# Out layer 0: the last weight quarter three steps behind the third instead of six

## The chip, the cores and the metric

One Trainium2 chip, one core. The metric is the device time of one execution in microseconds (us), the median of three runs. All times below are us from the start of the profiled execution's span, unless they are called a duration.

## What is computed

One inference step of a two-layer decoder trunk: 1024 prompt rows and 8 sample rows, width 1024, all in float32. Layer 0 mixes by stick-breaking attention and causal pooling, layer 1 by a Conformer convolution. Each layer ends in an output projection and a normalisation of the residual sum:

```python
h = concat([o_a * silu(g_a), o_b * silu(g_b)])      # layer 0's mixed rows, 1024 wide
x = layer_norm(ALPHA * x + h @ w_out, g, b)         # what is called "out layer 0" here
p = x @ w_in_c                                      # layer 1 begins with its input projection
```

The sample rows attend to 4096 cached positions each, through a page table. Their scores need one product of every cached K row with the query, spread over the whole of layer 0 as a background job.

## The kernel before

A projection is computed in three matmuls per block, because operands are split into a high part (float32r) and the rest: `XH` by `whi`, `XH` by `wlo`, `XL` by `whi`. TensorE (PE), VectorE (DVE), ScalarE (ACT) and GpSimd (POOL) run in the order in which the code issues their instructions (`manual_schedule` names these four). SyncE (SP), which issues all DMAs, is ordered by the framework's planner.

`out_layer` works in 32 steps. A step is a pair (weight quarter `n4`, row tile `tb`): 24 matmuls of 128x128 by 256 columns, then on DVE the residual sum (L1073) and its statistics (L1077). Steps 0 to 15 do quarters 0 and 1 for all tiles. After that quarter 2 runs over the tiles, and quarter 3 follows `lag` steps behind it:

```python
for i in range(NTB + lag):
    if i < NTB:
        order.append((2, i))
    if i >= lag:
        order.append((3, i - lag))
```

With `lag` 6 the steps from 16 on are (2,0) to (2,6), (3,0), (2,7), (3,1), (3,2) to (3,7). The two accumulators of PSUM alternate, so a step's matmuls wait until DVE has taken up the result of the step before the last.

The step of quarter 3 completes a row tile. Then:

- in the step itself, DVE aggregates the statistics (L1005) and POOL makes the reciprocal deviation `rs` (L1007, L1008);
- one step later (`DTC`) the normalisation `app`: two DVE instructions (L1015) against `gps0`, a copy of the gain in PSUM, one ACT scaling (L1031), one POOL addition of the bias (L1032), and a DMA of the rows to `x1_dram` (L1137). Tile 7 is normalised on DVE alone (L1024, L1025), in the same step as tile 6, with two PSUM banks of the `zt` ring as its place between;
- `FLAG` steps after that (3 for tiles 0 to 4) `fin0`: eight PE transposes (L1144) into two `zt` banks, and from there ACT (L195, `XH`) and DVE (L196, `XL`) make layer 1's operands.

`tail0` issues the loads of layer 1's first four weight blocks (`wraw`) at (3,2) to (3,5), and converts them at (3,4) to (3,7): ACT `whi` L205, POOL `wlo` L210. Quarter 3's own four blocks are loaded at steps 13 to 16 and converted at steps 16 to 19, whatever the lag.

After each step `tick(1)` moves the background job `decode_k` on by one unit: DVE reduces unit u-3 (L409), POOL or DVE multiplies unit u-2 (L417, every fourth one is DVE's), SP loads unit u (`kt`, L405, four buffers). Unit 63's multiplication stands in step 24, its reduction in step 25, the score transposes and ACT's four sigmoids (L429 to L434) in step 28, the two scans (L437, L440) in steps 29 and 30. So within a step the order on each engine is: conversion, step, statistics, `decode_k`, then what `point()` finds due.

Layer 1's input projection `c_gen` follows at once. Its first block needs `XH` and `XL` of tiles 0 to 3. After six of its matmuls come tile 4's transposes. The four `zt` banks of out layer 0 are replaced at that point by a pool with two (`swap_psum("pzc", 2)`).

Of the kernel before, what the change touches and what calls it, by code (L numbers as in the profile page):

```python
# [69 lines left out]
TSLOPE = 1.5  # L70
NHEADS = (0, 6, 6, 6, 6, 6, 6, 6)
SNY = 7
OLAGB = 6
FDMA = (2, 3, 4, 5)
FC = (4, 5, 6, 7)
FLAG = (3, 3, 3, 3, 3, 4, 6, 8)
# [24 lines left out]
def kernel(  # L101
# [33 lines left out]
    def psum(tag, bufs, shape=(P, 512), dt=F32):  # L135
        return (psq[0] if tag == "qv" else ps).tile(list(shape), dt, tag=tag, name=tag, bufs=bufs)
# [338 lines left out]
    def tick(n):  # L475
        while n > 0 and queue:
            try:
                next(queue[0])
                n -= 1
            except StopIteration:  # L480
                queue.pop(0)
# [626 lines left out]
    def load_res(tb):  # L1108
        if tb < NTB:
            sp.dma_start(X[tb], xp[tb * P:(tb + 1) * P, :])  # L1110

    def before0(n4, tb):
        if n4 == 0:
            load_res(tb + 2)
        if n4 == 0 and tb == 4:
            sp.dma_start(pool_sample[0, :, 0:PS_ - 1, :], state_pool[0, :, 1:PS_, :])
            sp.dma_start(conv_sample[0, :, 0:KS - 1, :], state_conv[0, :, 1:KS, :])
        if n4 == 1 and tb == 0:
            sp.dma_start(gb0[:, 0, :], ln_ab_g.to_broadcast([P, D]))
            sp.dma_start(gb0[:, 1, :], ln_ab_b.to_broadcast([P, D]))  # L1120
        if n4 == 2 and tb == 4:
            gps0.extend((psum("o", 1), psum("qv", 1)))
            for i in range(2):
                act.activation(out=gps0[i], in_=gb0[:, 0, i * 512:i * 512 + 512], func=AF.Copy)
# [11 lines left out]
    def fin0(tb, y, h):  # L1136
        sp.dma_start(x1_dram[tb * P:(tb + 1) * P, h], y[:, h])  # L1137

        def f():
            for hf in range(h.start // 512, h.stop // 512):  # L1140
# [10 lines left out]
    load_res(1)  # L1151
    out_layer(w_out0, first0, ahead0, X, [gb0], lnp, fin0,
              lambda n4, tb: tick(0 if n4 == 0 and tb < 4 else 2 if n4 == 1 and tb < 4 else 1), before0, None, tail0, OLAGB, FASTB, WIDE, gps0)
    def v_tile():
        return cd.tile([P, HW], F32, tag="vt", name="vt", bufs=VB)
# [553 lines left out]
```

## Time and profile before

| what | value |
|---|---|
| device time, median of 3 runs | 1108.89 us (1107.83 to 1113.12) |
| the profiled execution: its own time, its span | 1105.15 us, 1103.4 us |
| PE busy | 1038.9 us, 94% of the span |
| DVE busy | 827.3 us, 75% |
| POOL busy | 628.5 us, 57% |
| ACT busy | 493.3 us, 45% |
| DMA | 235.20 MB, mean 213 GB/s |

The span is the time from the first to the last instruction on the chip. Shares of the whole span average over stages with different limits; the change touches steps 18 to 28 of out layer 0, which lie between some 523 and 557 us, and what follows them.

### The profile page before, as it was taken

What the parts mean: (1) busy time and instruction counts of PE and PEld (TensorE: products, weight loads), DVE (VectorE), ACT (ScalarE), POOL (GpSimd) and SP (SyncE); (2) the same over time, 40 slices, a digit from 0 to 9 for tenths busy, and PEclk for the clock granted to TensorE, in tenths of its full rate; (3) what the DMA queues carried; (4) which work ended last, traced back from release to release, by engine and by line L of the source; (5) the groups of instructions that cost most, each with busy time, mean ns of one, the idle gap of its engine ahead of it and who ended that gap; (6) DMA issues with size and microseconds to landing.
All of it is one profiled execution on the core that took longest, in us unless ns stands there. A gap on an engine that the chain in (4) does not pass through costs nothing.

```text
span 1103.4 us, 19870 instructions
## 1 busy us (share of the span) xinstructions
PE 1038.9 (94%) x6804; PEld 835.9 (76%) x6804; DVE 827.3 (75%) x982; ACT 493.3 (45%) x933; POOL 628.5 (57%) x490
## 2 busy tenths in 40 slices
PE   8999999999999999989978999999999899789996
PEld 7998888888889788979966665567566466677785
DVE  3468998899578979678882799999999950584246
ACT  5355675575765567601162244535542412462211
POOL 3366867665266778768683276647754612342135
PEclk9999999999999899989989999999999999999998
DMA  8678767865357676487534886876787688386923
GB/s 266 202 216 237 249 193 221 251 181 177 115 157 215 201 261 209 152 293 246 168 136 143 256 256 213 262 246 201 214 262 241 205 246 266 109 282 216 333 96 135
DMA packets 179350, 235.20 MB, mean 213 GB/s; under 512 B 15434, under 2 KB 95955, under 8 KB 179225
## 3 DMA queue, kind: packets, MB, share of 16 engines
q1 hardware_dynamic: 179249, 233.94, 67.1%
q8 instruction: 53, 0.87, 0.3%
q14 instruction: 48, 0.39, 0.1%
HBM read 212.60 MB, written 16.14 MB: 207 GB/s over the span
## 4 chain that ended last, share of the span: by engine, by line
PE 50%; DVE 9%; POOL 8%; DMA 7%; issue 5%; ACT 3%; SPq 2%; POOLq 0%; DVEq 0%; ACTq 0%
PE acc L225 11%; PE acc L227 10%; PE acc L226 10%; PE qv L1169 6%; DMA kt<-in_cache_k_dram 3%; POOL kt L417 3%; DVE zw L409 2%; POOL wlo L210 2%; DVE kp L365 2%; PE o L865 2%; PE acc L1040 1%; DMA vt<-in_cache_v_dram 1%; PE qv L1205 1%; PE zt L849 1%; DVE kt L417 1%
## 5 line engine op out<-in xcount | busy, mean ns | idle before, releaser
L225 PE MATMUL acc<-xh,whi 128*128 128x384 f32 (+2 forms) x960 | 360.9, 376 | 9.3 <-ACT xh L195 6.4
L227 PE MATMUL acc<-xl,whi 128*128 128x384 f32 (+2 forms) x960 | 339.7, 354 | 0.5 <-DVE xl L196 0.5
L226 PE MATMUL acc<-xh,wlo 128*128 128x384 f32 (+2 forms) x960 | 339.4, 354 | 0.0
L417 POOL TENSOR_TENSOR kt<-kt,qbs 128x1024 f32<-128x1024 f32 x96 | 232.7, 2434 | 78.5 <-DMA kt<-in_cache_k_dram 66.2
L210 POOL TENSOR_TENSOR wlo<-wraw,whi 128x512 fp32r<-128x512 f32 x124 | 167.7, 1356 | 168.9 <-ACT whi L205 163.6
L1391 DVE SCALAR_TENSOR_TENSOR conv_acc<-hbuf,wdwT,conv_acc 128x1024 f32<-128x1024 f32 x196 | 252.8, 1290 | 6.8
L225 PEld LDWEIGHTS acc<-xh,whi 128*128 128x128 f32 x960 | 183.2, 191 | 76.0 <-issue 25.7
L227 PEld LDWEIGHTS acc<-xl,whi 128*128 128x128 f32 x960 | 183.1, 191 | 18.5 <-DVE xl L196 1.1
L226 PEld LDWEIGHTS acc<-xh,wlo 128*128 128x128 f32 x960 | 183.8, 191 | 16.1 <-POOL wlo L210 0.2
L409 DVE TENSOR_REDUCE zw<-kt 128x16 f32<-128x1024 f32 x128 | 153.1, 1212 | 31.6 <-POOL kt L417 26.5
L1381 POOL TENSOR_TENSOR conv<-conv,tap 128x512 f32<-128x512 f32 x84 | 105.9, 1294 | 17.9 <-ACT tap L1378 17.9
L205 ACT ACTIVATE whi<-wraw 128x512 fp32r<-128x512 f32 x126 | 77.6, 625 | 72.4 <-DMA wraw<-in_w_out_ab_dram 53.3
L1040 PE MATMUL acc<-whi,xh 128*128 128x256 f32 x352 | 102.7, 292 | 5.0 <-DVE xres L1073 4.9
L1042 PE MATMUL acc<-whi,xl 128*128 128x256 f32 x352 | 99.7, 283 | 2.4 <-DVE xl L196 2.4
L1041 PE MATMUL acc<-wlo,xh 128*128 128x256 f32 x352 | 99.7, 283 | 1.1 <-POOL wlo L210 1.0
L365 DVE TENSOR_TENSOR_SCAN kp<-kp,zt 128x512 f32<-128x512 f32 (+3 forms) x96 | 92.6, 964 | 3.0 <-ACT zt L361 2.9
L1378 ACT ACTIVATE tap<-hbuf,wdwT 128x512 f32<-128x512 f32 x84 | 59.7, 721 | 48.3 <-POOL conv L1381 38.4
L1169 PE MATMUL qv<-vt,zw 128*32 128x512 f32 x512 | 75.0, 604 | 4.6 <-DMA vt<-in_cache_v_dram 4.6
L1040 PEld LDWEIGHTS acc<-whi,xh 128*128 128x128 f32 x352 | 67.1, 190 | 13.7 <-issue 7.4
L360 ACT ACTIVATE kp<-zt,nbiash 128x512 f32<-128x512 f32 (+3 forms) x96 | 55.8, 581 | 46.1 <-PE zt L827 24.4
L1042 PEld LDWEIGHTS acc<-whi,xl 128*128 128x128 f32 x352 | 67.1, 191 | 2.6 <-DVE xl L196 2.6
L1041 PEld LDWEIGHTS acc<-wlo,xh 128*128 128x128 f32 x352 | 67.1, 191 | 1.5 <-POOL wlo L210 1.5
(287 smaller groups left out, 1488.1 us busy)
## 6 DMA issues: line engine op xcount, KB each, us to landing
kt<-in_cache_k_dram SPq DMA_DIRECT2D x256, 256.0 KB
vt<-in_cache_v_dram SPq DMA_DIRECT2D x256, 256.0 KB
wraw<-in_w_in_c_dram SPq DMA_DIRECT2D x48, 256.0 KB
vt<-in_w_in_c_dram SPq DMA_DIRECT2D x48, 256.0 KB
wraw<-in_w_in_ab_dram SPq DMA_DIRECT2D x46, 256.0 KB
xt<-in_x_prompt_dram SPq DMA_DIRECT2D x8, 512.0 KB
wraw<-in_w_out_ab_dram SPq DMA_DIRECT2D x16, 256.0 KB
xres<-in_x_prompt_dram SPq DMA_DIRECT2D x8, 512.0 KB
```

The source lines that it names most:

```text
L210: (eng or gp).tensor_tensor(out=lo, in0=raw, in1=hi.bitcast(F32), op=ALU.subtract)
L225: pe.matmul(o, hi[:, k % 4, :], xh, start=(k == 0), stop=False)
L226: pe.matmul(o, lo[:, k % 4, :], xh, start=False, stop=False)
L227: pe.matmul(o, hi[:, k % 4, :], xl, start=False, stop=(k == NK - 1))
L365: dve.tensor_tensor_scan(out=kr, data0=kr, data1=z[:, 0:1].broadcast_to([P, n]), initial=1.0 if prev is None else prev, op0=ALU.mult, op1= ...
L409: dve.tensor_reduce(out=seg[:, j // 8, j % 8:j % 8 + 2, bi * 8:bi * 8 + 8], in_=kts.pop(s - KLAG - 1).rearrange("p a (h d) -> p a h d", d=DH),
L417: eng.tensor_tensor(out=kt, in0=kt, in1=qrow[b], op=ALU.mult)
L1040: pe.matmul(o, XH[:, k, cs], hi[:, k % 2, :], start=(k == 0), stop=False)
L1041: pe.matmul(o, XH[:, k, cs], lo[:, k % 2, :], start=False, stop=False)
L1042: pe.matmul(o, XL[:, k, cs], hi[:, k % 2, :], start=False, stop=(k == NK - 1))
L1169: pe.matmul(pv[32 * bi:32 * bi + 32, :], Z[:, j % 8 * 4 + j // 8, :], vts[bi], start=(j == 0), stop=(j == NPG - 1), tile_position=(0, 32 * ...
L1391: dve.scalar_tensor_tensor(out=part[1], in0=hb[:, j:j + S], scalar=w, in1=part[1], op0=ALU.mult, op1=ALU.add)
```

## The change

The lag of out layer 0 becomes 3. The steps from 16 on are now (2,0) to (2,3), (3,0), (2,4), (3,1), (2,5), (3,2), (2,6), (3,3), (2,7), (3,4) to (3,7). Steps 28 to 31 hold the same pairs as before. (3,0), (3,1), (3,2) and (3,3) move from steps 23, 25, 26 and 27 to 20, 22, 24 and 26. The normalisations of tiles 0 to 3 come at the ends of steps 21, 23, 25 and 27 instead of 24, 26, 27 and 28, that of tile 4 stays at 29, and the transposes of tiles 0 to 3 come at the ends of steps 24, 26, 28 and 30 instead of 27, 29, 30 and 31. The first two loads of layer 1's weights are issued in steps 24 and 26 of the code instead of 26 and 27. The copy of the gain to PSUM moves from (2,4), which was step 20, to (2,2), which is step 18, so that it still stands ahead of the first normalisation. `decode_k` keeps its place, one unit after each step.

```diff
-OLAGB = 6
+OLAGB = 3
...
-        if n4 == 2 and tb == 4:
+        if n4 == 2 and tb == 2:
             gps0.extend((psum("o", 1), psum("qv", 1)))
             for i in range(2):
                 act.activation(out=gps0[i], in_=gb0[:, 0, i * 512:i * 512 + 512], func=AF.Copy)
```

## Rows read from the trace of the kernel before

**Rows 1.** Busy us of each engine by stretch, granted clock, DMA share, GB/s.
```profile
536.00:548.00 12.00, 12.00 (x104) 12.00 (x103) 9.98 (x16) 0.00 (x0) 7.93 (x5) 1.00 0.41 142
...
573.00:580.00 7.00, 3.48 (x10) 2.52 (x10) 5.78 (x11) 4.51 (x8) 6.83 (x9) 0.66 0.62 216
```
**Rows 2.** Timeline, PE: start, duration, line, output and inputs, idle before and releaser.
```profile
574.74 0.80 PE L225 MATMUL acc<-xh,whi 128*128 128x512 f32 x1 [5.95 <-ACT xh L195]
...
580.02 0.66 PE L1144 MATMUL zt<-ident,xres 128*128 128x128 f32 x4 [1.79 <-DVE xres L1025]
```
**Rows 3.** Chain that ended last, in order of time, around the end of out layer 0.
```profile
574.04 2.37 POOL xres L1032
576.41 1.25 POOL wlo L210
...
577.93 0.58 POOL rs L1008
578.56 1.42 DVE xres L1025 x2
...
584.36 0.40 PE acc L225
584.76 0.24 PE acc L226
```
**Rows 4.** Timeline, POOL.
```profile
530.49 1.28 POOL L210 TENSOR_TENSOR wlo<-wraw,whi 128x512 fp32r<-128x512 f32 x1
531.74 2.39 POOL L417 TENSOR_TENSOR kt<-kt,qbs 128x1024 f32<-128x1024 f32 x1
537.27 4.76 POOL L417 TENSOR_TENSOR kt<-kt,qbs 128x1024 f32<-128x1024 f32 x2 [3.14 <-DMA kt<-in_cache_k_dram]
```
**Rows 5.** Timeline, DVE.
```profile
536.43 0.41 DVE L1073 SCALAR_TENSOR_TENSOR xres<-xres,acc 128x256 f32<-128x256 f32 x1
...
537.23 1.20 DVE L409 TENSOR_REDUCE zw<-kt 128x16 f32<-128x1024 f32 x1
...
546.52 1.22 DVE L417 TENSOR_TENSOR kt<-kt,qbs 128x1024 f32<-128x1024 f32 x1
547.65 0.74 DVE L1015 SCALAR_TENSOR_TENSOR xres<-xres,mv,o 128x512 f32<-128x512 f32 x1
...
548.97 0.41 DVE L1073 SCALAR_TENSOR_TENSOR xres<-xres,acc 128x256 f32<-128x256 f32 x1
...
549.88 0.26 DVE L1005 BATCH_NORM_AGGREGATE mv<-st 128x2 f32<-128x24 f32 x1
...
564.96 1.29 DVE L196 TENSOR_TENSOR xl<-zt,xh 128x512 fp32r<-128x512 f32 x2 [1.39 <-ACT xh L195]
...
568.64 1.21 DVE L440 TENSOR_TENSOR_SCAN kpd<-kpd 128x512 f32<-128x512 f32 x1
```
**Rows 6.** Timeline, ACT.
```profile
559.17 1.28 ACT L433 ACT_TABLE_LOAD   x1
560.47 0.69 ACT L433 ACTIVATE kpd<-zt,nbiasd 128x512 f32<-128x512 f32 x1
...
562.76 1.17 ACT L1031 ACTIVATE xres<-xres,rs 128x1024 f32<-128x1024 f32 x1
563.80 0.64 ACT L205 ACTIVATE whi<-wraw 128x512 fp32r<-128x512 f32 x1
564.33 1.10 ACT L195 ACTIVATE xh<-zt 128x512 fp32r<-128x512 f32 x2
```
**Rows 7.** Timeline, POOL, then DVE: a DVE multiplication while POOL multiplies.
```profile
510.44 2.40 POOL L417 TENSOR_TENSOR kt<-kt,qbs 128x1024 f32<-128x1024 f32 x1 [0.90 <-DMA kt<-in_cache_k_dram]
...
511.03 2.90 DVE L417 TENSOR_TENSOR kt<-kt,qbs 128x1024 f32<-128x1024 f32 x1
```
**Rows 8.** Timeline, SP: DMA issues.
```profile
528.19 4.00 SPq L200 DMA_DIRECT2D wraw<-in_w_in_c_dram  x2
532.78 6.52 SPq L405 DMA_DIRECT2D kt<-in_cache_k_dram  x8
```

## The prediction

> **What bounds the kernel now.** I read the page first, then the busy time by stretch, the timelines of PE, DVE, POOL, ACT and SP from 505 to 600 us, and the chain that ended last. PE is busy 94% of the span, but that is a mean. Up to about 548 us PE has no idle time in out layer 0, and DVE is already at 83% of it, with `decode_k` beside it [rows 1]. The end of the stage is another place: from 573 to 580 PE has 3.48 us of 7, at a granted clock of 0.66, while POOL has 6.83 and DVE 5.78 [rows 1]. PE waits 5.95 us for tile 3's `XH`, then 1.79 us for L1025, tile 7's last step on DVE [rows 2]. The chain says why L1025 is late: POOL adds tile 5's bias, makes a `wlo`, makes tile 7's `rs`, and only then can L1025 run [rows 3]. So what counts is when L1025 ends, 579.98 now; layer 1 follows from there, with PE on the chain.
>
> The tile 4 transposes that wait for it (580.02) don't read tile 7. They use a `zt` bank, and the pool of two that has just replaced the pool of four lays its second bank over the one that L1025 reads. The change makes as many `zt` allocations in the same order at the end (tiles 2 and 3, then tile 7), so I take this wait to stay.
>
> **The change part by part.** No instruction is added or removed. The sum is a walk through the four fixed orders: an instruction starts when its engine is free and its input is done (0.06 us later, the rows' usual distance). Durations, start to start: result and statistics 0.8 us (536.43 to 537.23) [rows 5], with aggregation 1.05; reduction 1.15; normalisation on DVE 1.32 (two L1015), on ACT 1.15, on POOL 2.38; `xl` pair 1.21; scan 1.21; `rs` pair 0.85 (end of `wlo` to end of `rs`); `wlo` 1.27; POOL's multiplication 2.38, DVE's 1.15 [rows 3 to 6]. Walked with them, the old order ends L1025 at 579.8, row 579.98; that is the error that I claim for the method where nothing new enters.
>
> *Weights and the gain.* Quarter 3's last `wlo` ends at 531.77 [rows 4]. (3,0) is now step 20, which starts at 529.0 and wants this block after three quarters of its 2.86 us, at 531.2: 0.6 us of PE, inside DVE's lag (its next result is taken up at 536.4), so it costs nothing. ACT waits for loads around steps 16 to 20, and the two copies of the gain fall into that at no cost. If that cover were gone they would cost some 1.2 us (512 columns each, as the `whi` of 0.64) [rows 6].
>
> *Tile 0's normalisation now meets `decode_k`.* Up to 538.35 DVE and POOL go as in the old rows [rows 4, 5]. Then DVE normalises tile 0 to 539.7, ACT to 540.9, POOL adds to 543.3 and does tile 1's `rs` to 544.15. Behind them in POOL's queue stands the multiplication of unit 61, which used to start at 539.65, the second of the two in its row [rows 4]. It now ends at 546.5, and DVE, in order, has to wait for it with its reduction, having nothing left since 542.65: 3.9 us of DVE idle. POOL itself stood idle from 539.6 to 540.9 for ACT. This is the core of my forecast: a normalisation crosses DVE, ACT and POOL, and what is queued behind its last part on POOL is the work that DVE needs next. In the old order it came at step 24, when POOL's last multiplication was past.
>
> *Tile 1's meets DVE's last multiplication.* DVE goes on: reduction to 547.7, tile 1's normalisation to 549.05, result and aggregation to 550.1, reduction to 551.25, then unit 63's multiplication, while POOL adds tile 1's bias from 550.3 to 552.7. A DVE multiplication alone took 1.22 us [rows 5]; one that began inside a POOL multiplication took 2.90 and ended 1.07 after POOL's did [rows 7]. The same here would end it at 553.8 instead of 552.4: 1.4 us. Below, 0 if a bias addition doesn't do what a multiplication does; above, the whole 1.68 between the two rows. I take 1.4, since both are POOL instructions of two SBUF operands and 2.4 us. The Trainium skill, SBUF — State Buffer, section "SBUF: two separate sides", has this as an exclusive lock of a port pair between a DVE operation with two SBUF inputs and a GpSimd operation that reads SBUF, whichever starts first. The 2.90 agrees. By that page the 1.4 us is due, without it the sum is 1.4 less.
>
> *Steps 24 to 28.* Tile 0's `xl` to 555.0, step 25's result to 555.8, the last reduction to 556.95, tile 2's normalisation to 558.3, step 26 to 559.3, tile 1's `xl` (after ACT) 560.05 to 561.3, step 27 to 562.1, tile 3's normalisation to 563.4, step 28 to 564.45. PE waits for DVE's results meanwhile, some 2 us at step 26 and under 1 us at steps 27 to 31.
>
> *The sigmoids.* In step 28 ACT has tile 3's scaling to 564.6, the table load to 565.9 and four sigmoids (2.29 us) to 568.2 [rows 6]. Tile 2's transposes now come in this step, so `xh` is behind the sigmoids, `xl` behind `xh`, and everything on DVE behind `xl`, which starts at 568.8: 4.3 us idle. In the old rows the same block held up tile 1's `xl`, with 1.39 us of DVE idle [rows 5], since tile 3's normalisation and a scan lay ahead of it.
>
> *The end.* DVE from 568.8 has no idle time to speak of: `xl`, step 29, scan, tile 4's normalisation to 573.6; step 30, scan, tile 3's `xl` to 577.15, tile 5's normalisation to 578.5. Tile 5 passes ACT at 579.7 and POOL at 582.1, `wlo` is at 583.4, tile 7's `rs` at 584.2, L1025 ends at 585.65, and the transposes start at 585.7. That is **5.7 us later** than 580.02 (4.3 without the port's 1.4). What was moved out of the end, one normalisation and one `xl` of DVE (2.5 us), is more than used up by the waits.
>
> *Clock.* After the 5.95 us idle PE ran at 0.43 us a matmul of 512 columns, the lower level (1.2 GHz), until 584.4, then at 0.24 [rows 2, 3]. Now it idles about 3.5 us before layer 1 and 6.6 before the tile 4 transposes. As long a slow stretch after 585.7 as there was after 574.74 (9.6 us instead of the 3.9 left after 580.5) costs 5.7 x (1 - 0.24/0.43) = 2.5 us more; none, if it lasts only as long as before. I take the middle, 1.3.
>
> *Moved DMAs.* The rows of tiles 0 to 3 are written earlier; their writes become ready after all K loads, so I leave them behind these in SP's queue. Layer 1's first weight loads already stand ahead of the last K loads in SP's queue, and held them to 532.78 [rows 8]; waiting for the same `wlo` as before, they cost the same.
>
> **Sum.** 4.3 + 1.4 + 1.3 = 7.0 us, 0.6%. The profiled execution took 1105.15 (span 1103.4 and 1.75 around it), so 1112.15 like for like; the median of the runs stands 3.7 above it, so 1115.9. The likeliest case's own range is 4.3 + 0 + 0 to 4.3 + 1.7 + 2.5: 1113.2 to 1117.4.
>
> **Rivals.** *The spacing pays* (the other side): DVE loses neither 3.9, 1.4 nor 4.3 us, as would be if POOL and ACT were done in time at steps 23 to 28. For it: two steps are 5.7 us, and a tile needs 3.2 of POOL and 2.5 of DVE. Against it: the queues are fixed and unit 61 stands behind tile 0. L1025 would come 3.9 us early, the slow stretch costs up to 1.7 less: 1108.9 - 3.9 - 1.3 = 1103.7. It decides once unit 61's multiplication starts by 540.
>
> *Nothing arrives at the end*: later stages take up the delay, for instance where K's successor, the V pages, sets the pace. For it: the chain passes a few V loads, 3 to 4 us each. Against it: PE stands on the chain from 580 on. 1108.9.
>
> *SP reorders*: tile 0's write, ready at 543.3, is put ahead of K unit 61's load. That unit would land some 4.4 us later, at 547.8 instead of being waited for until 544.15: 3.7 us more, 1119.6. Against it: every K load is free to go before that write is.
>
> **Chances.** Forecast 0.52, of which 0.36 above the bound (the sum lies 1.5 us beyond it) and 0.16 below; SP reorders 0.13; nothing arrives 0.20; spacing pays 0.15, about half of it beyond the bound. 0.5% of the time, 5.5 us, is about what a measurement of this kernel tells from no change. Slower 0.49, within 0.43, faster 0.08. The range goes from 1105.5, which leaves out most of the case that pays, to 1120.5, past the SP case.
>
> **What would show it.** In the changed profile: POOL's L1032 of tile 0 between two multiplications of units 60 and 61, and a DVE idle near 4 us before L409 at about 546; a DVE multiplication near 2.6 us around 551; a DVE wait of about 4 us for ACT's `xh` in step 28, near 568; PE's tile 4 transposes waiting for L1025 until about 585.7. It is wrong if unit 61 isn't behind tile 0, if the wait for L1025 is gone (`zt` banks laid otherwise), or if the end comes before 580.

## The result: 1117.09 us, 0.84% slower

| | before | after |
|---|---|---|
| device time, median | 1108.89 us (1104.20 to 1113.12, 7 runs) | 1117.09 us (1113.59 to 1121.08, 7 runs) |
| ratio of the runs, as recorded (the medians alone give 1.0074) | | 1.0084, 95% interval 1.0065 to 1.0102 |
| profiled execution: span | 1103.4 us | 1114.5 us |

The two profiled executions differ ahead of the change already: quarter 3's last `wlo`, from the same instructions, ends at 531.77 before [rows 4] and at 534.59 after. So I count from there below: **after minus 2.8 us** is the forecast's own time.

Busy time by stretch, after (busy us of PE, PEld, DVE, ACT, POOL, granted clock, DMA share, GB/s):
```profile
536.00:548.00 12.00, 12.00 (x104) 12.00 (x104) 9.08 (x15) 1.15 (x1) 8.16 (x8) 1.00 0.67 226
548.00:556.00 8.00, 6.16 (x42) 5.96 (x42) 6.42 (x8) 2.12 (x3) 6.45 (x4) 0.84 0.05 20
...
580.00:590.00 10.00, 2.44 (x13) 1.63 (x12) 7.12 (x13) 4.01 (x6) 9.83 (x11) 0.71 0.40 148
```
From 536 to 548 PE still has no idle time, as before [rows 1]. From 548 to 556 it has 6.16 of 8 us at a granted clock of 0.84, where before it had 7.10 at 1.00. At the end it has 2.44 of 10.

POOL, after (the timelines show start, duration, engine, line, operation, then idle time before and what ended it):
```profile
539.80 2.41 POOL L417 TENSOR_TENSOR kt<-kt,qbs 128x1024 f32<-128x1024 f32 x1 [1.99 <-DMA kt<-in_cache_k_dram]
...
543.88 2.40 POOL L1032 TENSOR_TENSOR xres<-xres,lngb 128x1024 f32<-128x1024 f32 x1 [1.68 <-ACT xres L1031]
...
547.09 4.72 POOL L417 TENSOR_TENSOR kt<-kt,qbs 128x1024 f32<-128x1024 f32 x2
553.37 2.38 POOL L1032 TENSOR_TENSOR xres<-xres,lngb 128x1024 f32<-128x1024 f32 x1 [1.55 <-ACT xres L1031]
...
577.96 3.15 POOL L1032 TENSOR_TENSOR xres<-xres,lngb 128x1024 f32<-128x1024 f32 x1 [1.95 <-ACT xres L1031]
```
DVE, after:
```profile
549.51 1.22 DVE L409 TENSOR_REDUCE zw<-kt 128x16 f32<-128x1024 f32 x1 [4.00 <-POOL kt L417]
...
554.13 2.69 DVE L417 TENSOR_TENSOR kt<-kt,qbs 128x1024 f32<-128x1024 f32 x1
...
571.89 1.29 DVE L196 TENSOR_TENSOR xl<-zt,xh 128x512 fp32r<-128x512 f32 x2 [4.41 <-ACT xh L195]
...
587.61 1.41 DVE L1025 SCALAR_TENSOR_TENSOR xres<-zt,rs,lngb 128x512 f32<-128x512 f32 x2 [2.36 <-POOL rs L1008]
```
The two K multiplications that stood back to back after 537.27 [rows 4] are apart: tile 0's addition lies between, after a POOL idle of 1.68 for ACT, and DVE waits 4.00 for unit 61. Then come the stretched multiplication (2.69) and the wait behind the sigmoids (4.41). In ACT's queue the table load and four sigmoids stand ahead of tile 2's `xh`, as forecast:
```profile
567.65 1.28 ACT L433 ACT_TABLE_LOAD   x1
568.95 0.69 ACT L433 ACTIVATE kpd<-zt,nbiasd 128x512 f32<-128x512 f32 x1
...
571.24 1.10 ACT L195 ACTIVATE xh<-zt 128x512 fp32r<-128x512 f32 x2
```
PE, after:
```profile
578.93 0.50 PE L225 MATMUL acc<-xh,whi 128*128 128x512 f32 x1 [2.27 <-DVE kpd L440]
...
589.08 1.12 PE L1144 MATMUL zt<-ident,xres 128*128 128x128 f32 x4 [7.26 <-DVE xres L1025]
```
The waits of [rows 2] have changed places: less ahead of layer 1 (2.27 instead of 5.95), more ahead of tile 4's transposes (7.26 instead of 1.79). The chain that ended last, after, shows when the clock came back:
```profile
590.41 0.43 PE acc L225
...
594.25 0.39 PE acc L225
594.64 0.23 PE acc L226
```

**One measure for all runs.** The runs of one kernel scatter by some 10 us. Distances inside the stage can be told apart better. I take two in each profile, from the end of quarter 3's last `wlo`: to the end of L1025, and to the start of the first score transposes in layer 1 (eight, PE, L467), which lie behind the slow stretch of the clock. Each is read from one profiled execution, but where two kernels are alike they repeat: after, e3 and e8 do the same up to L1025 but for the place of the gain's copy, and have 54.43, 54.49 and 54.44 us; e1 and e4 have 51.40 and 51.47. At L467 after and e8 are 0.35 us apart.

| | to L1025, us | against before | to L467, us | against before | ratio as recorded (95%) |
|---|---|---|---|---|---|
| before | 48.21 | | 60.75 | | |
| after | 54.43 | +6.2 | 67.78 | +7.0 | 1.0084 (1.0065 to 1.0102) |
| e1_rest_later | 51.40 | +3.2 | 64.97 | +4.2 | 1.0050 (1.0027 to 1.0073) |
| e2_xh_first | 52.13 | +3.9 | 65.43 | +4.7 | 1.0042 (1.0017 to 1.0067) |
| e3_tile4_later | 54.49 | +6.3 | 66.27 | +5.5 | 1.0071 (1.0046 to 1.0097) |
| e4_both | 51.47 | +3.3 | 62.28 | +1.5 | 1.0024 (1.0003 to 1.0044) |
| e5_lag6_no_mul | 46.69 | -1.5 | 58.83 | -1.9 | 0.9982 (0.9956 to 1.0007) |
| e6_lag3_no_mul | 47.76 | -0.4 | 61.11 | +0.4 | 0.9997 (0.9972 to 1.0022) |
| e7_lag4 | 54.47 | +6.3 | 66.98 | +6.2 | 1.0070 (1.0042 to 1.0098) |
| e8_gain_copy_later | 54.44 | +6.2 | 68.13 | +7.4 | 1.0102 (1.0058 to 1.0145) |
| e9_lag6_tile4_later | 48.51 | +0.3 | 59.54 | -1.2 | 0.9979 (0.9957 to 1.0001) |
| e10_tile1_apart | 55.82 | +7.6 | 68.54 | +7.8 | 1.0075 (1.0048 to 1.0102) |
| e11_all_lag3 | 55.62 | +7.4 | 67.54 | +6.8 | 1.0070 (1.0034 to 1.0105) |
| e12_no_mul63 | 51.80 | +3.6 | 65.00 | +4.3 | 1.0049 (1.0025 to 1.0072) |

11 us are 1%, so the fifth column lies within the interval of the last one in every row but that of after, which is 0.2 us below its own.

### The profile page after: what moved, and what is told of

It reads as the page before. It is cut to its first block, busy times and chain, and to the rows that moved or that the text cites. A ratio compares the mean times of both kernels' runs of the same rounds, so it can differ in the third digit from the quotient of the medians.

```text
span 1114.5 us, 19868 instructions
## 1 busy us (share of the span) xinstructions
PE 1043.1 (94%) x6804; PEld 836.5 (75%) x6804; DVE 828.7 (74%) x982; ACT 493.4 (44%) x933; POOL 631.2 (57%) x490
## 4 chain that ended last, share of the span: by engine, by line
PE 42%; DVE 9%; POOL 8%; DMA 6%; issue 5%; ACT 4%; SPq 2%; POOLq 0%; DVEq 0%; ACTq 0%
PE acc L225 9%; PE acc L227 8%; PE acc L226 8%; PE qv L1169 6%; DMA kt<-in_cache_k_dram 3%; POOL kt L417 2%; DVE zw L409 2%; POOL wlo L210 2%; PE qv L1205 1%; DVE xl L196 1%; DVE kp L365 1%; PE zt L1040 1%; DMA vt<-in_cache_v_dram 1%; PE acc L1040 1%; ACT conv L1601 1%
## 5 line engine op out<-in xcount | busy, mean ns | idle before, releaser
L417 POOL TENSOR_TENSOR kt<-kt,qbs 128x1024 f32<-128x1024 f32 x96 | 232.4, 2431 | 86.7 <-DMA kt<-in_cache_k_dram 71.9
```

The costliest lines, as they stand in the source:

```text
L417: eng.tensor_tensor(out=kt, in0=kt, in1=qrow[b], op=ALU.mult)
```

## The experiments

The theory: tile 0's addition stands ahead of unit 61 in POOL's queue and costs DVE 4 us, tile 1's stretches unit 63, and both reach L1025. The main rival to this cause: (3,0) and the transposes come earlier and meet weights and operands that are late (PE does wait 1.51 us for a `wlo` there), whatever `decode_k` does. The row after, PE:
```profile
534.65 0.39 PE L1041 MATMUL acc<-wlo,xh 128*128 128x256 f32 x1 [1.51 <-POOL wlo L210]
```

### The multiplications taken out of both orders

```diff
-                    eng.tensor_tensor(out=kt, in0=kt, in1=qrow[b], op=ALU.mult)
+                    if hf == 0 or s - KLAG < 60:
+                        eng.tensor_tensor(out=kt, in0=kt, in1=qrow[b], op=ALU.mult)
```
In the kernel before (e5):

> The kernel before (lag 6) with the last four multiplications of the background job left out (units 60 to 63 of the second half are reduced unmultiplied). Worked out with the rows' durations, L1025 ends 2.1 us earlier than in the kernel before: some 1106 us. It is the partner of the next run; alone it says little.

In the changed kernel (e6):

> The changed kernel (lag 3) with the same four multiplications left out. Queue theory (tile 0's addition ahead of unit 61 on POOL, unit 63 on DVE under tile 1's addition): the two causes that need these multiplications are gone, and only the sigmoids ahead of tile 2's XH are left; worked out, L1025 ends 1.4 us later than with lag 6 and the same omission, so the difference of the pair falls from 7 to 9 us to 1 to 3: 1107 to 1109 us. Rival (late weights of quarter 3, earlier transposes, moved DMAs): the pair stays 7 to 9 us apart, 1113 to 1115 us.

Medians 1108.34 and 1108.36 us, against 8.2 us between the full kernels. At L1025 6.2 us of difference shrink to 1.1, at L467 7.0 to 2.3. So the order of quarter 3 alone costs 1.1 to 2.3 us in the stage (1.4 was expected for the sigmoids), too little for the medians to tell; the other 5 us need the meeting with units 60 to 63. (e5 itself was expected 2.1 us earlier at L1025 and came 1.5 earlier; its median is 1108.34, not 1106.) No run takes unit 61's wait away by itself.

The rival falls, and the places in the traces say so more sharply than e6, whose PE happens not to wait for that `wlo`. In e12, below, PE waits only 0.23 us for it, in e3 not at all, and DVE's wait for unit 61 is 4.01 and 4.00 all the same; L1025 comes at 54.49 in e3 and at 54.43 in after. PE, e12 (its lines from 416 on stand one further down):
```profile
537.66 0.39 PE L1042 MATMUL acc<-wlo,xh 128*128 128x256 f32 x1 [0.23 <-POOL wlo L210]
```

### Unit 63 alone

```diff
-                    eng.tensor_tensor(out=kt, in0=kt, in1=qrow[b], op=ALU.mult)
+                    if hf == 0 or s - KLAG != 63:
+                        eng.tensor_tensor(out=kt, in0=kt, in1=qrow[b], op=ALU.mult)
```

> The changed kernel with unit 63's multiplication alone left out in the second half of the cached positions (its K rows are reduced unmultiplied, so those scores are other numbers); it is the DVE multiplication that took 2.69 us under POOL's addition for tile 1, where one alone takes 1.22. Units 60 to 62 and with them the wait of 4.00 us stay. If the 2.69 is real time on DVE's queue, taken by the shared port, DVE is 2.6 us earlier from there and keeps that to the end of the stage, since the sigmoids hang on tile 3's normalisation: L1025 ends 3.6 us later than in the kernel before, counted from quarter 3's last wlo, instead of 6.2; the time is about 1114.5. If the long duration is only where the profile puts a wait that exists anyway, DVE wins 1.2 us or nothing: L1025 5.0 to 6.2 us later, the time 1116 to 1117. The two times are closer than the runs can tell; the places in the trace decide.

L1025 came 3.6 us later than before, L467 4.3, the median was 1114.2. L1025 is 2.6 us earlier than in after, so all but 0.1 of the 2.69 us was real time on DVE's queue, and 1.5 of it is more than the 1.22 of one alone. The wait for unit 61 was still there (DVE, e12; L418 is L417):
```profile
552.52 1.22 DVE L409 TENSOR_REDUCE zw<-kt 128x16 f32<-128x1024 f32 x1 [4.01 <-POOL kt L418]
```

### POOL's half of a normalisation one step later

```diff
-                    for h in halves:
-                        norm_b(gb[0], y, rs, fast, h)
-                        finish(tb, y, h)
+                    def rest():
+                        for h in halves:
+                            norm_b(gb[0], y, rs, fast, h)
+                            finish(tb, y, h)
+                    if fast0 is FASTB and tb < 4:
+                        defer(1, rest)
+                    else:
+                        rest()
...
-        defer(FLAG[tb], f)
+        defer(FLAG[tb] - (tb < 4), f)
```

> Changed kernel, but for tiles 0 to 3 ACT's scaling and POOL's bias addition are issued one step after the two DVE instructions of the normalisation; the transposes stay where they are. Queue theory (what the normalisation leaves on POOL stands ahead of the K multiplications that DVE needs next): unit 61's multiplication is ahead of tile 0's addition, DVE's wait there falls from 4.0 us to about 1.5, unit 63's DVE multiplication is back at 1.2 us from 2.7, and tile 2's XH comes earlier, so that tile 7's L1025 ends about 5.5 us earlier than in the changed kernel: 1111 to 1112 us, at most 3 us above before. Rival (quarter 3's weights are wanted before they are ready, PE waits 1.5 us in its first step, and loses the rest to the earlier transposes): nothing of that is touched, 1117 us.

1112.25 us, half of the loss back: L1025 comes 3.0 us earlier than in after, not 5.5, and unit 63's multiplication is not back at 1.2. DVE, e1:
```profile
547.96 1.22 DVE L409 TENSOR_REDUCE zw<-kt 128x16 f32<-128x1024 f32 x1 [1.50 <-POOL kt L417]
...
553.75 3.11 DVE L417 TENSOR_TENSOR kt<-kt,qbs 128x1024 f32<-128x1024 f32 x1
...
570.84 2.41 DVE L437 TENSOR_TENSOR_SCAN kpd<-kpd 128x512 f32<-128x512 f32 x1
```
and POOL, e1:
```profile
553.39 2.39 POOL L1032 TENSOR_TENSOR xres<-xres,lngb 128x1024 f32<-128x1024 f32 x1
...
569.77 2.40 POOL L1032 TENSOR_TENSOR xres<-xres,lngb 128x1024 f32<-128x1024 f32 x1 [2.11 <-PE acc L1042]
572.12 2.22 POOL L210 TENSOR_TENSOR wlo<-wraw,whi 128x512 fp32r<-128x512 f32 x1
```
With unit 61 ahead of the addition the 4.00 is gone, and two shorter waits (1.50 and 1.03) take its place. The collisions moved with the additions: unit 63 now takes 3.11, and a scan that took 1.16 takes 2.41.

### Tile 2's transposes ahead of the sigmoids

```diff
-            between(n4, tb)
-            point()
+            if fast0 is FASTB and (n4, tb) == (3, 4):
+                point()
+                between(n4, tb)
+            else:
+                between(n4, tb)
+                point()
```

> Changed kernel, but in step 28 tile 2's transposes and their XH, XL are issued ahead of the score transposes and the four sigmoids. Queue theory: DVE's wait of 4.4 us for ACT before tile 2's XL shrinks to under 1 us, but the scan then waits for the sigmoids; worked out with the durations of the rows, L1025 ends 2.3 us earlier than in the changed kernel: 1114 to 1115 us. Rival (late weights, earlier transposes): 1117 us.

At both places 2.3 us back, as worked out; the median, 1112.4 us, is lower than the 1114 to 1115 expected, within the scatter of the runs. The wait of 4.41 in step 28 shrank to 0.67 (DVE, e2):
```profile
566.26 1.29 DVE L196 TENSOR_TENSOR xl<-zt,xh 128x512 fp32r<-128x512 f32 x2 [0.67 <-ACT xh L195]
```

### Tile 4's transposes behind L1025

```diff
-FLAG = (3, 3, 3, 3, 3, 4, 6, 8)
+FLAG = (3, 3, 3, 3, 6, 6, 6, 8)
```
In the changed kernel (e3):

> Changed kernel, but tiles 4 and 5 are transposed later: after 24 and after 30 of layer 1's matmuls instead of 6 and 18 (FLAG 6 and 6 instead of 3 and 4). Queue theory, end part (PE stands idle 7.3 us because the second half of tile 4's transposes lies on the bank that L1025 reads): PE does 18 more matmuls in that wait, which are worth 4.2 us at the higher clock: 1112 to 1113 us, with L1025 ending where it does now. If the wait is for tile 4's own rows or for the weights, or if the end of the stage is not on the path: 1117 us.

1116.0 us: a miss. PE, e3:
```profile
595.71 1.97 PE L1144 MATMUL zt<-ident,xres 128*128 128x128 f32 x8 [3.90 <-DVE xres L1025]
598.95 0.26 PE L455 MATMUL zt<-ident,crow 1*128 1x1 f32 x1 [1.28 <-POOL crow L451]
```
PE's wait shrinks from 7.26 to 3.90 us, but the eight transposes run at 1.97 us where eight took 1.03 at the upper clock, and a new wait of 1.28 for `crow` follows. The granted clock is 0.50 from 594.3 to 604.5, until 8.8 us after these transposes began; in after it is back 5.4 us after they began. L1025 doesn't move; 1.5 us are left of the 3.4 saved.

Together with the later half (e4, both edits):

> The first and the third of these together. Queue theory: layer 1 begins about 3 us earlier than in the kernel before (571.7 against 574.7 by the rows' durations) and no longer stands for L1025: 4 to 6 us faster than before, 1103 to 1105 us. If either gain is only the other's waiting time in another place, no better than the better one of the two, 1111 us.

1110.57 us, a miss again. At L467 5.5 us come back, more than the 2.8 and 1.5 singly, but it is still 1.5 us later than before, where 4 to 6 us earlier was expected. Against that forecast layer 1 still stands for L1025, which is 3.3 us late (PE, e4; L1150 is L1144):
```profile
590.34 1.97 PE L1150 MATMUL zt<-ident,xres 128*128 128x128 f32 x8 [3.92 <-DVE xres L1025]
```

In the kernel before (e9):

> The kernel before (lag 6) with tiles 4 and 5 transposed after 24 and 30 of layer 1's matmuls (FLAG 6 and 6). The wait for L1025 there is 1.79 us and is filled; the 5.95 us before layer 1's first matmul and the slow clock after them stay. Queue theory: 1.8 to 2.5 us faster than before, 1106 to 1107.5 us. If filling that wait only moves it to the accumulators or to tile 4's and 5's own XH and XL: the same as before.

1106.59 us, ratio 0.9979 (0.9957 to 1.0001), 1.2 us less at L467. Of the versions that do all the work it has the lowest median, but it is not clear of no change.

### Lag 4

```diff
-OLAGB = 3
+OLAGB = 4
```

> Lag 4, everything else as in the changed kernel. Queue theory: tile 0's normalisation comes one step later, behind unit 61 and ahead of unit 62, and unit 63 doesn't meet an addition; worked out, L1025 ends 1.8 us later than with lag 6 instead of 5.7 to 6.2, with little on top for the clock: 1110 to 1111.5 us. Rival (late weights): the first step of quarter 3 still comes one step earlier than its last block by the old order's slack, but has 2.9 us more than with lag 3, so the wait of 1.5 us is gone; all of the loss should go with it, 1109 us.

1116.77 us: a miss. The walk had tile 0 ahead of unit 62, and still put L1025 only 1.8 us later; the wait for unit 62 is as long as unit 61's was, 3.98 us. POOL, then DVE, then PE, then the windows of e7:
```profile
549.92 2.39 POOL L1032 TENSOR_TENSOR xres<-xres,lngb 128x1024 f32<-128x1024 f32 x1 [1.53 <-ACT xres L1031]
...
553.12 2.38 POOL L417 TENSOR_TENSOR kt<-kt,qbs 128x1024 f32<-128x1024 f32 x1
```
```profile
555.54 1.22 DVE L409 TENSOR_REDUCE zw<-kt 128x16 f32<-128x1024 f32 x1 [3.98 <-POOL kt L417]
...
573.81 2.64 DVE L437 TENSOR_TENSOR_SCAN kpd<-kpd 128x512 f32<-128x512 f32 x1
```
```profile
559.59 0.58 PE L1040 MATMUL acc<-whi,xh 128*128 128x256 f32 x1 [3.29 <-DVE xres L1073]
```
```profile
556.00:560.00 4.00, 0.70 (x5) 0.50 (x4) 3.97 (x6) 0.70 (x1) 0.00 (x0) 0.81 0.00 0
560.00:565.00 5.00, 5.00 (x25) 5.00 (x25) 4.59 (x9) 1.68 (x4) 3.15 (x3) 0.50 0.25 105
```
PE runs dry for 3.29 us and then works five us at 0.50, busy throughout but with 25 matmuls where PE does 45 in five us of e11 at the full clock; DVE, late until then, has to wait for PE (1.30 and 1.28 us). A scan behind a POOL addition (2.64) comes on top. The same queue, one unit further on.

### The gain's copy back at (2,4)

```diff
-        if n4 == 2 and tb == 2:
+        if n4 == 2 and tb == 4:
```

> The changed kernel with its second edit undone: the gain is copied to PSUM ahead of (2,4), now step 21, instead of (2,2), step 18. Queue theory: ACT has 13 us of idle time there either way, no change, 1116 to 1118 us. If the copy at step 18 held up quarter 3's last conversion on ACT and so the first step of quarter 3: 1 to 2 us faster than the changed kernel, 1115 us.

1118.73 us in 4 runs, 0.7 above what was expected and within their scatter; L1025 at 54.44 as after. The second edit of the change costs nothing that shows here.

### Tile 1's addition out of unit 63's way

e10 is e1 with
```diff
-                        defer(1, rest)
+                        defer(3 if tb == 1 else 1, rest)
...
-        defer(FLAG[tb] - (tb < 4), f)
+        defer(FLAG[tb] - (tb < 4) - (tb == 1), f)
```

> The first experiment (rest of the normalisation one step later) with tile 1's rest two steps later still, behind step 26's rs on POOL, and tile 1's transposes one step later, so that POOL's addition of tile 1 no longer runs beside unit 63's DVE multiplication (3.11 us there). If the two engines keep each other off: the multiplication is back at 1.2 us and the stage 1 to 2 us shorter than with the first experiment, 1110 to 1111.5 us. If 3.11 us has another cause (operands, data of the DMA), or DVE has that much slack: the multiplication stays near 3 us, or the time at 1112 us.

e11 is e10 with the edits of e2 and e3:

> Lag 3 with all that helped it: rest of the normalisation later, tile 1 apart, tile 2's XH ahead of the sigmoids, tiles 4 and 5 transposed later. If the losses of the parts are separate, some 3 us less than the first and third together (1110.6): 1106 to 1108 us, not slower than before. If they are mostly the same wait seen in several places: 1110 us.

1119.8 and 1115.51 us, two misses. Unit 63 does run alone (DVE, then POOL, then PE, e11):
```profile
550.48 1.22 DVE L417 TENSOR_TENSOR kt<-kt,qbs 128x1024 f32<-128x1024 f32 x1
```
```profile
557.29 0.22 POOL L1007 TENSOR_SCALAR rs<-mv 128x1 f32<-128x1 f32 x1 [7.16 <-DVE mv L1005]
...
558.12 4.67 POOL L1032 TENSOR_TENSOR xres<-xres,lngb 128x1024 f32<-128x1024 f32 x2
```
```profile
560.53 1.97 PE L1154 MATMUL zt<-ident,xres 128*128 128x128 f32 x8 [3.88 <-POOL xres L1032]
```
But tile 1's addition now stands in POOL's queue behind tile 3's `rs`, which waits 7.16 us for DVE's statistics, and the transposes (L1154 here) stand in PE's queue one step behind the addition. PE runs ahead of DVE: it stood 3.88 us at these transposes (2.37 in e10), and the clock was 0.50 from 560 to 565. I had freed POOL and not looked at PE's place in its own queue.

## Why the prediction was right

- **Unit 61 behind tile 0.** 3.9 us of DVE idle forecast at about 546; 4.00, up to 549.51 (546.7 with the offset taken off). POOL's idle for ACT and the order of the queue are those of the forecast. Most of the loss hangs on this step and the next: without units 60 to 63's multiplications 1.1 of the 6.2 us at L1025 are left. Of the 5.1 that go, unit 63's stretch is 1.5; the rest, some 3.6, is an inference by difference, not a run of its own.
- **Unit 63 under tile 1's addition.** 1.4 us forecast; 2.69 against 1.22 is 1.5, and e12 shows that it is paid in full. The forecast's row [rows 7] was one case in which DVE's multiplication ended, by the row, 1.09 us after POOL's. The others agree: in after unit 63 ends at 556.82, POOL's addition at 555.75, 1.07 earlier; in e1 1.08 for the multiplication, and 1.08 for the scan; in e7 1.09 for the scan. Wherever in POOL's operation DVE began, it ended about one own duration (1.16 to 1.22) after POOL. The Trainium skill, SBUF — State Buffer, section "SBUF: two separate sides", has the exclusive lock of the port pair that this amounts to, and these rows agree.
- **Sigmoids.** 4.3 us forecast, 4.41 measured. Moving the transposes ahead of them gave back 2.3 us, so a good half of this wait was on the path. In e6, with DVE early, a wait of 3.87 is still there, and L1025 is only 1.1 us later than in e5, its partner: that a wait is long doesn't make it a price. DVE, e6:
```profile
567.32 1.29 DVE L196 TENSOR_TENSOR xl<-zt,xh 128x512 fp32r<-128x512 f32 x2 [3.87 <-ACT xh L195]
```
- **The end.** L1025 5.7 us later forecast, 6.2 measured. 0.3 is there by DVE's `xl` in step 28 (571.89, less the offset 569.07, for 568.8). The rest is on POOL: tile 4's addition takes 3.15, beginning under DVE's scan of 577.71, so that tile 5's, behind a `wlo` and tile 6's `rs`, starts at 583.16 and not, as forecast, at 579.7 (582.5 with the offset). I had used 2.38 for every addition, though the kernel before has one of 3.11, under the scan at 568.64 [rows 5] (POOL, before):
```profile
568.89 3.11 POOL L1032 TENSOR_TENSOR xres<-xres,lngb 128x1024 f32<-128x1024 f32 x1 [0.39 <-ACT xres L1031]
```
- **Clock.** 1.3 us forecast, about 0.8 measured: from L1025's 6.2 to 7.0 at L467. PE idles 2.27 us before layer 1, not 3.5. The forecast took the slow time before as one stretch from layer 1's first matmul to 584.4. By the granted clock it was interrupted (two windows of before, then one of after):
```profile
577.80:581.20 3.40, 1.61 (x12) 1.10 (x11) 2.76 (x5) 1.79 (x4) 3.32 (x5) 1.00 0.69 237
581.20:584.60 3.40, 3.40 (x10) 2.64 (x9) 0.69 (x1) 0.25 (x2) 2.95 (x11) 0.50 0.83 270
```
```profile
584.30:594.40 10.10, 5.32 (x15) 4.35 (x16) 3.65 (x6) 2.14 (x5) 9.43 (x19) 0.50 0.57 194
```
So behind L1025 PE worked 3.4 us at the lower level before, and some 5.4 after (589.08 to 594.5). 2.0 us more, times 1 - 0.24/0.43 as in the forecast, is 0.9. The middle between no stretch and a full one was too much.
- **Weights.** PE waits 1.51 us for the `wlo` of (3,0), not 0.6; as forecast that sets nothing: DVE takes up the next step's result 4.66 us after the end of that `wlo` in both orders (536.43 before [rows 5], 539.25 after), and the K multiplication at 539.80 waits 1.99 for its load.
- **Sum.** 7.0 us forecast and 7.0 measured from `wlo` to L467. The mechanism is the one forecast; that the figures agree so closely is luck, since L1025's part was 0.5 us too small and the clock's 0.5 too large. The medians differ by 8.2, and the ratio's interval is about 7.2 to 11.3 us (0.65% to 1.02%); what the last 1.2 us are is not shown. The profiled executions also end 1.2 us further behind the start of L467 (512.1 and 510.9 us), but one execution of each says little on that.
- **The rivals.** *Spacing pays* asked for unit 61 to start by 540; it started at 547.09 (544.3 with the offset taken off). *Nothing arrives* is out, the delay stays to the end. *SP reorders*: POOL's pair at 547.09 waits for no DMA.

What stays open: whether lag 3 can be made as fast as 6. The edits that remove one collision made another each time (e1, e7, e10, e11), and an order in which neither POOL's queue nor PE's catches one was not found in these runs.

## What to carry to other kernels

When engines run in program order, a step that crosses three of them (DVE, ACT, POOL here) holds back whatever is queued behind its last part, for as long as its slowest input is late: read, for each moved step, the next instruction in each queue that it passes and who waits for that. Spreading work evenly over time gains nothing if the even places are those where another engine's queue is full; a burst in a place that is already waiting can be the cheaper one. Walk every queue, PE's too, for each repair as for the change: of the five misses in time here, e10 and e11 came from a walk that left PE's queue out, and e7's walk had the order right and the wait too short.

## What was not expected of the hardware

DVE's scans took longer beside POOL's additions, as multiplications did (2.41 and 2.64 us for 1.16 to 1.22), and POOL's operations beside DVE's: in after a 128x1 operation of POOL took 1.00 us under a scan, where it took 0.22 elsewhere:
```profile
574.35 1.00 POOL L1007 TENSOR_SCALAR rs<-mv 128x1 f32<-128x1 f32 x1
```
PE ran at the lower of its two clock levels (1.2 instead of 2.4 GHz) behind an idle time in the middle of a stage: 3.29 us idle in e7 and 3.88 in e11, and a granted clock of 0.50 in the five us after, so that a wait on DVE came back as a wait for PE. How long one idle time is doesn't settle it: after 1.84 us idle at 552.43 in after the clock was 0.50 from 553.6 to 556.9, while in e2 it stayed at 1.00 after 1.86 us, and in e1 after 2.48.
